# Down weights read two rows to a partition, quarter columns for a lightest expert of up to 32 tokens, and a gather and a code block moved

## The chip, the cores and the metric

One core of a Trainium2 chip runs the whole program. The metric is device time in microseconds (us) of one execution, taken as the median of several. A core has a matrix engine (TensorE, PE in the profile; its weight loads are PEld), a vector engine (DVE), a scalar engine (ACT), GpSimd (POOL) and SyncE (SP), which here issues the weight loads as DMAs. Each engine works through its own list of instructions in order and waits for the others by semaphores.

## The reference, cut to what matters

Two layers act on 256 latent and 256 context tokens of width 1024. The part that the change touches is the channel mixer of the second layer, a SwiGLU with 8 experts of which each of the 256 latent tokens takes two:

```
logits = h @ w_router                       # h: 256 x 1024
top_v, top_i = lax.top_k(logits, 2)
gates = softmax(top_v) spread over the 8 experts, 0 elsewhere
for e in range(8):
    g, u = split(h @ w_gu[e])               # w_gu[e]: 1024 x 7168
    y += gates[:, e:e+1] * ((silu(g) * u) @ w_down[e])   # w_down[e]: 3584 x 1024
```

All is in 32-bit floats. The weights of the 8 experts are 352 MB and are read once.

## The kernel before

The first layer and the attention of the second come first; then the router's logits are made, the experts are sorted by their number of tokens (`sort_experts`; expert 0 is always put first), and `posms` and `gates` hold places and gates by rank. The code then branches. If any expert has more tokens than its rank allows (`odd > 0`), a general path runs (`any_experts`); otherwise `run_pairs` runs. In it the four ranks 0, 2, 3, 1 are "heavy" (up to 128 tokens, `HS`) and ranks 4, 5, 6, 7 are "light" (up to 64 tokens, `LS`), and `schedule` interleaves a heavy and a light one, chunk by chunk: the hidden width 3584 is cut into three chunks of 1024 and one of 512 (`CHUNKS`), and the light one runs one chunk behind. For a chunk there are gate and up products (`Hg`, `Hu`, `Lg`, `Lu`), a transposition of the activations (`Ht`, `Lt`), and in the next slot the down product (`Hd`, `Ld`). The list is cut where rank 1 begins: plan 0 is ranks 0, 2, 3 with 4, 5 and most of 6, plan 1 is rank 1 with the end of 6 and with 7. Between the plans is a second branch: with `k1` over 128 tokens in rank 1, plan 1 runs in its "few" form, in which tokens 129 to 160 of rank 1 are a third group (`few_tokens` gathers them, L1711 and L1781 are its products, 32 columns wide).

Weights come in tiles of 1 MB through a ring of 8 buffers (`raw`), by SP in one queue, in the order of use; SP issues a load when the buffer that it takes is free (L80). A heavy tile is split into a high and a low part by ACT (`whi`, L99) and DVE (`wlo`, L100), three split tiles at most, and takes three products per piece (L537 to L539). A light tile goes into PE unsplit (L1735 gate and up, L1801 down). There two instructions of 64 tokens work side by side on two halves of a chunk's columns. In plan 1 a heavy buffer comes free only after the few product has read it, since `Wb.keep` holds it.

A down tile is 256 rows of 1024 floats, put as rows p and 128+p into partition p. `heavy_turn` and `light_turn` transpose blocks of 128 neighbouring columns of the activations, which are the weights of the down products.

Gathers and the adding of finished experts into `y` (`combine`, L1363) are generators in `bg`, of which a step is run after most operations. The order on PE, DVE and ACT is that of the code in `run_pairs`.

Of the kernel before, what the change touches and what calls it, by code (L numbers as in the profile page):

```python
# [8 lines left out]
F32 = mybir.dt.float32  # L9
# [158 lines left out]
def kernel(ctx: ExitStack, tc: tile.TileContext, x, c, cx, c_ctx, w_ada, b_ada, norm_g,  # L168
# [890 lines left out]
    def pair_items(plan):  # L1059
        r = []  # L1060
        for op, p, c, i in plan:
            l = "l" if op[0] == "L" else "m"
            f0, n = CHUNKS[c]
            for t in range(2 * i, 2 * i + 2):
                if op[1] == "d":
                    f = f0 + 256 * t
                    r.append((tile_of(p, slice(f, f + 256), slice(0, D), w_dn_m, "o (f p) n -> p (o f) n"), l + "d", 2))
                elif op[1] in "gu":
                    q, k = f0 + (FF if op[1] == "u" else 0), 2048 // n
                    r.append((tile_of(p, slice(128 * k * t, 128 * k * t + 128 * k), slice(q, q + n), w_gu_m,  # L1070
                                      "o (k p) n -> p (o k) n"), l + "g", k))
        return r
# [545 lines left out]

    def light_gather(p):
# [29 lines left out]
    def run_pairs(plan, few, todo):  # L1649
# [14 lines left out]
        def few_tokens(p):  # L1664
            sl2 = x2r[:, 0:256].rearrange("p (t n) -> p t n", t=2)
            for t in range(2):
                p2 = tiny([128, 1], "p2")
                V.tensor_scalar(p2, posms[:, t, p:p + 1], -128.0, None, op0=OP.add)
                V.tensor_scalar(sl2[:, t, :].rearrange("p (g n) -> p g n", g=4),
                                iota[:, 0:32].unsqueeze(1).to_broadcast([128, 4, 32]), p2, None, op0=OP.is_equal)  # L1670
            for h in range(2):
                pb, q = hb[h], slice(32 * h, 32 * h + 32)
                for i, (t, src) in enumerate(((0, hth), (0, htl), (1, hth), (1, htl))):
                    PE.matmul(pb, sl2[:, t, :], src[:, t, hsl(h)], start=i == 0, stop=i == 3)
                A.copy(fact[q, :], pb[q, :])
            yield
            pb = tr0[:, 0:256]
            for c in range(4):
                PE.transpose(pb[:, 64 * c:64 * c + 64], fact[0:64, 128 * c:128 * c + 128], ident[0:64, 0:64])
            A.copy(x2.rearrange("p (h c) n -> p c h n", h=2), pb.rearrange("p (c h n) -> p c h n", c=4, h=2))  # L1680
            for t in range(2):
                PE.transpose(facc[:, 128 * t:128 * t + 128], sl2[:, t, :].bitcast(F32), ident)
            A.copy(st2, facc[:, :256])
            yield

        def heavy_gu(p, c, i, up):
            x1, n = XG[p], CHUNKS[c][1]
            nb, w4, per = n // 512, n // 4, 2048 // n
            tokens = few_tokens(p) if few and c == i == 0 and not up else None
            if tokens:  # L1690
                next(tokens)
# [10 lines left out]
            if tokens:  # L1702
                next(tokens)
# [21 lines left out]

        def light_gu(p, c, i, up):
            n = CHUNKS[c][1]
            w2, per = n // 2, 2048 // n
            o = lb[:, 0:w2]
            for t in range(2 * i, 2 * i + 2):  # L1730
                raw = Wb.get("lg")
                for k in range(per):
                    kk = per * t + k
                    for g_ in range(2):
                        PE.matmul(o[64 * g_:64 * g_ + 64, :], X32[p][:, kk, :], raw[:, k, w2 * g_:w2 * g_ + w2],  # L1735
                                  start=kk == 0, stop=kk == KD - 1)
            if i == n // 512 - 1:
                evac(1, [lact[:, 0:w2]], [o], up)

        def heavy_turn(p, c, i):  # L1740
            n = CHUNKS[c][1]
            for b in range(n // 512):
                for k in range(4):
                    q = slice(128 * k, 128 * k + 128)
                    PE.transpose(hb[b][:, q], hact[b][:, q], ident)
                A.copy(th[b], hb[b])
                V.tensor_tensor(tl[b], hb[b], th[b].bitcast(F32), op=OP.subtract)
            if few and p == 1:
                for j in range(n // 512):
                    PE.transpose(tr0[:, 128 * j:128 * j + 128], fact[:, 128 * j:128 * j + 128], ident)  # L1750
                A.copy(t2[:, 0:n // 4], tr0[:, 0:n // 4])

        def light_turn(p, c, i):
            w2 = CHUNKS[c][1] // 2
            for j in range(w2 // 128):
                PE.transpose(lb[:, 128 * j:128 * j + 128], lact[:, 128 * j:128 * j + 128], ident)
            A.copy(lt[:, 0:w2], lb[:, 0:w2])  # L1757
# [35 lines left out]
        def light_down(p, c, i):  # L1793
            nj = CHUNKS[c][1] // 256
            final = c == len(CHUNKS) - 1
            for t in range(2):
                raw = Wb.get("ld")
                for f in range(2):
                    g_, j = divmod(4 * i + 2 * t + f, nj)
                    for h in range(2):  # L1800
                        PE.matmul(lacc[64 * h:64 * h + 64, :], lt[:, 128 * j + 64 * g_:128 * j + 64 * g_ + 64],  # L1801
                                  raw[:, f, hsl(h)], start=c == 0 and i == t == f == 0, stop=final and t == 1 and f == 1)
            if final:
                o = [ring.tile([128, 512], F32R, "x2", i) for i in range(2)]
                split_hl(*o, lacc)
                S_["parts"] = [(SL32[p], in_halves(o))]
# [81 lines left out]
    with odd_arm.Else():  # L1888
# [58 lines left out]
```

## Time and profile before

| | us |
|---|---|
| median of 3 runs (1916.24 to 1918.6) | 1918.11 |
| the profiled execution | 1916.19 |
| its span in the trace | 1914.4 |
| PE busy | 1818.3 (95%) |
| DVE busy | 948.4 (50%) |
| ACT busy | 812.2 (42%) |

Engines overlap, so busy times don't add up to the span. A view of windows gives for each stretch its length, then the busy time and count of instructions of PE, PEld, DVE, ACT and POOL, the granted clock of PE (1.00 is the full 2.4 GHz, 0.5 is 1.2 GHz), the busy share of the 16 DMA engines and the GB/s moved. A share over 1 comes from packets that overlap on an engine. A timeline row is start, duration, engine, line, operation, output and inputs, shapes, count of merged instructions, and in brackets the idle time ahead and what ended it. A wait row is who waited for whom, the total, the times and the longest. A row for one line of the code gives least, median and greatest duration in ns. A q behind an engine means its sequencer.

### The profile page before, as it was taken

The numbers are of one execution on the slowest core, as the hardware profiler recorded it, in microseconds if no ns is written. First come the engines' busy times: TensorE is split into PE (matmuls) and PEld (weight loads), VectorE is DVE, ScalarE is ACT, GpSimd is POOL, SyncE is SP. The second block draws the span as 40 slices with busy tenths as digits, with TensorE's granted clock in tenths as the row PEclk, the third lists the DMA queues.
The fourth block names the chain that finished last, engine by engine and source line by source line (L and its number), as shares of the span: only waits on it lengthen the run. The fifth ranks groups of instructions, "written<-read, shape, count | busy, mean of one in ns | idle before, by whom it ended". The sixth has DMA issues, their size and how long they took to land. (4 is left out here: it accounts for less than half of the span.)

```text
span 1914.4 us, 23955 instructions
## 1 busy us (share of the span) xinstructions
PE 1818.3 (95%) x9321; PEld 1273.7 (67%) x9321; DVE 948.4 (50%) x1310; ACT 812.2 (42%) x1194; POOL 79.0 (4%) x139
## 2 busy tenths in 40 slices
PE   6999999999999999999779999999999996999997
PEld 3866679877777888877666656566565653655553
DVE  3344578322232748536556545665455543545433
ACT  3354457221212547438445535454354443434322
POOL 2200110000000000200200000000000000000001
PEclk9999999999999999999969999999999998999999
DMA  9956286645552656733438999999999998898994
GB/s 337 200 174 203 105 287 209 208 154 176 172 179 89 220 180 235 174 104 111 176 107 339 368 404 404 409 409 406 406 404 409 410 404 349 323 375 334 373 376 187
DMA packets 223760, 521.12 MB, mean 272 GB/s; under 512 B 30040, under 2 KB 83856, under 8 KB 223632
## 3 DMA queue, kind: packets, MB, share of 16 engines
q1 hardware_dynamic: 223152, 519.27, 74.3%
q8 instruction: 77, 1.26, 0.3%
q14 instruction: 51, 0.42, 0.1%
q10 hardware_dynamic: 480, 0.18, 0.0%
HBM read 518.31 MB, written 3.13 MB: 272 GB/s over the span
## 5 line engine op out<-in xcount | busy, mean ns | idle before, releaser
L100 DVE TENSOR_TENSOR wlor<-rawr,whir 128x1024 fp32r<-128x1024 f32 x336 | 395.7, 1221 | 386.3 <-ACT whir L99 375.0
L99 ACT CAST whir<-rawr 128x1024 fp32r<-128x1024 f32 x336 | 335.4, 1049 | 340.9 <-DMA rawr<-in_w_gu_moe_dram 163.1
L100 DVE TENSOR_TENSOR wlo<-raw,whi 128x1024 fp32r<-128x1024 f32 x188 | 224.6, 1222 | 113.6 <-ACT whi L99 74.5
L99 ACT CAST whi<-raw 128x1024 fp32r<-128x1024 f32 x192 | 193.0, 1049 | 143.8 <-PE pg L538 40.3
L1735 PE MATMUL gur<-rawr,x32r 128*64 128x512 f32 (+1 forms) x1024 | 205.1, 547 | 6.5 <-ACT lar L1757 5.3
L537 PE MATMUL gur<-whir,xgr 128*128 128x512 f32 x448 | 181.0, 404 | 11.8 <-issue 6.7
L538 PE MATMUL gur<-wlor,xgr 128*128 128x512 f32 x448 | 176.0, 393 | 0.0
L539 PE MATMUL gur<-whir,xgr 128*128 128x512 f32 x448 | 175.6, 392 | 0.0
L1735 PEld LDWEIGHTS gur<-rawr,x32r 128*64 128x64 f32 x1024 | 69.5, 137 | 118.2 <-issue 100.0
L537 PEld LDWEIGHTS gur<-whir,xgr 128*128 128x128 f32 x448 | 84.9, 190 | 51.1 <-issue 22.0
L1801 PE MATMUL pd<-rawr,lar 128*64 128x512 f32 x448 | 101.7, 598 | 0.5 <-ACT lar L1757 0.5
L539 PEld LDWEIGHTS gur<-whir,xgr 128*128 128x128 f32 x448 | 84.8, 189 | 18.4
L538 PEld LDWEIGHTS gur<-wlor,xgr 128*128 128x128 f32 x448 | 84.9, 189 | 16.0
L537 PE MATMUL pg<-hh,whi 128*128 128x512 f32 (+1 forms) x256 | 95.0, 372 | 0.0
L539 PE MATMUL pu<-hh,wlo 128*128 128x512 f32 (+1 forms) x256 | 93.0, 363 | 0.4 <-DVE wlo L100 0.4
L539 PE MATMUL pg<-hh,wlo 128*128 128x512 f32 (+1 forms) x256 | 93.1, 364 | 0.0
L537 PE MATMUL pu<-hh,whi 128*128 128x512 f32 (+1 forms) x256 | 92.9, 363 | 0.0
L538 PE MATMUL pg<-hl,whi 128*128 128x512 f32 (+1 forms) x256 | 92.9, 363 | 0.0
L538 PE MATMUL pu<-hl,whi 128*128 128x512 f32 (+1 forms) x256 | 92.8, 362 | 0.0
L945 DVE TENSOR_TENSOR act<-sg,pu 128x512 f32<-128x512 f32 (+1 forms) x32 | 19.8, 620 | 147.1 <-PE pu L539 128.7
L537 PE MATMUL py<-whi,ah 128*128 128x512 f32 x224 | 87.4, 390 | 0.0
L539 PE MATMUL py<-whi,al 128*128 128x512 f32 x224 | 86.8, 390 | 0.6 <-DVE al L550 0.6
(391 smaller groups left out, 2972.5 us busy)
## 6 DMA issues: line engine op xcount, KB each, us to landing
rawr<-in_w_gu_moe_dram SPq DMA_DIRECT2D x224, 1024.0 KB
rawr<-in_w_down_moe_dram SPq DMA_DIRECT2D x112, 1024.0 KB
raw<-in_w_ada_dram SPq DMA_DIRECT2D x48, 1024.0 KB
raw<-in_w_gu_dense_dram SPq DMA_DIRECT2D x32, 1024.0 KB
raw<-in_w_down_dense_dram SPq DMA_DIRECT2D x28, 1024.0 KB
raw<-in_w_in_dram SPq DMA_DIRECT2D x24, 1024.0 KB
raw<-in_w_out_dram SPq DMA_DIRECT2D x12, 1024.0 KB
BM<-rep SPq DMA_DIRECT2D x8, 512.0 KB
```

The source lines that it names most:

```text
L99: nc.scalar.copy(hi[:, q], flat[:, q])
L100: (nc.gpsimd if g == "G" else nc.vector).tensor_tensor(lo[:, q], flat[:, q], hi[:, q].bitcast(F32), op=OP.subtract)
L537: PE.matmul(o, wh, mh, start=first, stop=False, skip_group_check=shared)
L538: PE.matmul(o, wh, ml, start=False, stop=False, skip_group_check=shared)
L539: PE.matmul(o, wl, mh, start=False, stop=last, skip_group_check=shared)
L945: V.tensor_tensor(act[f // 4][:, f % 4, s0:s0 + n], sg, pu, op=OP.mult)
L1735: PE.matmul(o[64 * g_:64 * g_ + 64, :], X32[p][:, kk, :], raw[:, k, w2 * g_:w2 * g_ + w2], start=kk == 0, stop=kk == KD - 1)
L1801: PE.matmul(lacc[64 * h:64 * h + 64, :], lt[:, 128 * j + 64 * g_:128 * j + 64 * g_ + 64], raw[:, f, hsl(h)], start=c == 0 and i == t == f ...
```

## The change

1. Down tiles of the chunks of 1024 are read with rows 2p and 2p+1 in partition p, so that a partition's 8 KB is one stretch of memory. To match, the transpositions of those chunks take every second column of a 256-wide block (`block`), not 128 neighbouring ones.
2. If the lightest expert (rank 7) has at most 32 tokens (`k7`), plan 1 is run in a form in which its products use four groups of 32 instead of two of 64 (`groups`, `quarters`). Its gather of tokens is the same (`light_gather`); `quarter_slots` makes the scattering matrix for this form.
3. The gather of the few tokens (`few_tokens`, now `few_gather`) moves from inside the first heavy product of plan 1 to the background of plan 0, behind the gather of rank 7.
4. The branch on `odd` is laid out so that the general path is not the code that follows it.

```diff
-                    r.append((tile_of(p, slice(f, f + 256), slice(0, D), w_dn_m, "o (f p) n -> p (o f) n"), l + "d", 2))
+                    rows_ = "o (p f) n -> p (o f) n" if n == 1024 else "o (f p) n -> p (o f) n"
+                    r.append((tile_of(p, slice(f, f + 256), slice(0, D), w_dn_m, rows_), l + "d", 2))
...
+    LQ = ring.tile([128, 512], F32R, "x2", 3)[:, 0:256]
+
+    def quarter_slots(p):
+
+        sl = LQ.rearrange("p (t n) -> p t n", t=2)
+        for t in range(2):
+            V.tensor_scalar(sl[:, t, :].rearrange("p (g n) -> p g n", g=4),
+                            iota[:, 0:32].unsqueeze(1).to_broadcast([128, 4, 32]), posms[:, t, p:p + 1], None,
+                            op0=OP.is_equal)
+        yield from pause(2)
+        pb = tbank()
+        for t in range(2):
+            PE.transpose(pb[:, 128 * t:128 * t + 128], sl[:, t, :].bitcast(F32), ident)
+        A.copy(LQ, pb[:, :256])
+        yield
...
+    def few_gather(p):
+
+        sl2 = x2r[:, 0:256].rearrange("p (t n) -> p t n", t=2)
+        fact = ring.tile([128, 512], F32, "sg", 1)
+        for t in range(2):
+            p2 = tiny([128, 1], "p2")
+            V.tensor_scalar(p2, posms[:, t, p:p + 1], -128.0, None, op0=OP.add)
...
+        yield from pause(2)
+        for h in range(2):
+            pb, q = tbank(), slice(32 * h, 32 * h + 32)
+            for i, (t, src) in enumerate(((0, hth), (0, htl), (1, hth), (1, htl))):
+                PE.matmul(pb, sl2[:, t, :], src[:, t, hsl(h)], start=i == 0, stop=i == 3)
+            A.copy(fact[q, :], pb[q, :])
+            yield
...
-            tokens = few_tokens(p) if few and c == i == 0 and not up else None
-            if tokens:
-                next(tokens)
...
+        def groups(p):
+
+            return 4 if quarters and p == LS[-1] else 2
+
         def light_gu(p, c, i, up):
-            n = CHUNKS[c][1]
-            w2, per = n // 2, 2048 // n
-            o = lb[:, 0:w2]
+            n, G = CHUNKS[c][1], groups(p)
+            wg, per, m = n // G, 2048 // n, 128 // G
+            o = lb[:, 0:wg]
...
-                    for g_ in range(2):
-                        PE.matmul(o[64 * g_:64 * g_ + 64, :], X32[p][:, kk, :], raw[:, k, w2 * g_:w2 * g_ + w2],
+                    for g_ in range(G):
+                        PE.matmul(o[m * g_:m * g_ + m, :], X32[p][:, kk, 0:m], raw[:, k, wg * g_:wg * g_ + wg],
                                   start=kk == 0, stop=kk == KD - 1)
...
+        def block(a, c, k):
+
+
+            if CHUNKS[c][1] < 1024:
+                return a[:, 128 * k:128 * k + 128]
+            return a[:, 256 * (k // 2):256 * (k // 2) + 256].rearrange("p (n f) -> p f n", f=2)[:, k % 2, :]
...
-                    PE.transpose(hb[b][:, q], hact[b][:, q], ident)
+                    PE.transpose(hb[b][:, q], block(hact[b], c, k), ident)
...
-                        PE.matmul(lacc[64 * h:64 * h + 64, :], lt[:, 128 * j + 64 * g_:128 * j + 64 * g_ + 64],
-                                  raw[:, f, hsl(h)], start=c == 0 and i == t == f == 0, stop=final and t == 1 and f == 1)
+
+                        q = 64 * h + 32 * f if G == 4 else 64 * h
+                        PE.matmul(lacc[q:q + m, :], lt[:, 128 * j + m * g_:128 * j + m * g_ + m], raw[:, f, hsl(h)],
+                                  start=c == 0 and i == t == 0 and (f == 0 or G == 4),
+                                  stop=final and t == 1 and (f == 1 or G == 4))
...
+    k7 = nc.values_load(keyi[0:1, 7:8], min_val=0, max_val=8 * S + 7)
...
-    with tc.If(odd > 0) as odd_arm:
+    with tc.If(odd > 0, preferred_fallthrough_block=False) as odd_arm:
...
-            ("Hg", 2, 3, 0): [lambda: light_gather(6)], ("Hg", 3, 2, 0): [lambda: light_gather(7)]})
+            ("Hg", 2, 3, 0): [lambda: light_gather(6)], ("Hg", 3, 2, 0): [lambda: light_gather(7), lambda: quarter_slots(7), lambda: few_gather(1)]})
...
-            finish(gates[:, :, LS[-1]], run_pairs(plans[1], True, {}))
+            with tc.If(k7 < 8 * 33) as quarter_arm:
+                finish(gates[:, :, LS[-1]], run_pairs(plans[1], True, {}, True))
+            back1()
+            with quarter_arm.Else():
+                finish(gates[:, :, LS[-1]], run_pairs(plans[1], True, {}))
```

How this moves instructions is seen on PE at three places. At the branch on `odd`, PE's list before is this (L1350 is the last transposition of the first gather, L1880 the branch, L1596 the first line of the general path):

```order
L1350 MATMUL pd_7384<-kc,slr_7398 128x128 x2
L1875 TENSOR_LOAD bad
L1876 TENSOR_LOAD keyi
L1880 COMPARE_AND_BRANCH
L1596 TENSOR_LOAD cnt
L1599 COMPARE_AND_BRANCH
```

PE's list at the same branch (now L1913) in the changed kernel; L537 to L539 are the first products of plan 0:

```order
L1351 MATMUL pd_7384<-kc,slr_7398 128x128 x2
L1907 TENSOR_LOAD bad
L1908 TENSOR_LOAD keyi
L1909 TENSOR_LOAD keyi
L1913 COMPARE_AND_BRANCH
L537 MATMUL gur_7409<-whir_7102,xgr_7387 128x512
L538 MATMUL gur_7409<-wlor_7103,xgr_7387 128x512
```

Plan 0 now follows the branch directly, and a third register load, that of `k7`, stands ahead of it. At the branch between the plans PE's list before is this (L1756 is the last transposition of plan 0, L1674 the gather of the few tokens, L537 the first heavy product of rank 1):

```order
L1756 MATMUL gur_7411<-kc,sgr_7401 128x128 x4
L1895 COMPARE_AND_BRANCH
L1674 MATMUL gur_7409<-hth,x2r 128x512
L1674 MATMUL gur_7409<-htl,x2r 128x512
L1674 MATMUL gur_7409<-hth,x2r 128x512
L1674 MATMUL gur_7409<-htl,x2r 128x512
L1674 MATMUL gur_7410<-hth,x2r 128x512
L1674 MATMUL gur_7410<-htl,x2r 128x512
L1674 MATMUL gur_7410<-hth,x2r 128x512
L1674 MATMUL gur_7410<-htl,x2r 128x512
L537 MATMUL gur_7409<-whir_7216,xgr_7387 128x512
```

The same place in PE's list of the changed kernel, where L1784 is that transposition and L1928 and L1929 are the branches on `k1` and `k7`:

```order
L1784 MATMUL gur_7411<-kc,sgr_7401 128x128 x4
L1928 COMPARE_AND_BRANCH
L1929 COMPARE_AND_BRANCH
L537 MATMUL gur_7409<-whir_7216,xgr_7387 128x512
L538 MATMUL gur_7409<-wlor_7217,xgr_7387 128x512
```

The eight gather products are gone from between the branch and the first heavy product. In plan 1, at the first gate product of rank 7, PE's list before is this (L1711 is the few product, L1735 the light one):

```order
L539 MATMUL gur_7410<-whir_7102,xgr_7387 128x512
L1711 MATMUL tr_7382<-rawr_7090,x2f 32x256 x8
L1711 MATMUL tr_7382<-rawr_7092,x2f 32x256 x8
L1735 MATMUL gur_7411<-rawr_7094,x32r_7395 64x512 x4
L1735 MATMUL gur_7411<-rawr_7096,x32r_7395 64x512 x4
L537 MATMUL gur_7409<-whir_7216,xgr_7387 128x512
```

The same place in PE's list of the changed kernel, where L1728 is the few product and L1756 the light one:

```order
L539 MATMUL gur_7410<-whir_7102,xgr_7387 128x512
L1728 MATMUL tr_7382<-rawr_7090,x2f 32x256 x8
L1728 MATMUL tr_7382<-rawr_7092,x2f 32x256 x8
L1756 MATMUL gur_7411<-rawr_7094,x32r_7395 32x256 x8
L1756 MATMUL gur_7411<-rawr_7096,x32r_7395 32x256 x8
L537 MATMUL gur_7409<-whir_7216,xgr_7387 128x512
```

The light product has taken on the shape and count of the few product.

## Rows read from the trace of the kernel before

**Rows 1.** Windows: most of plan 0, two stretches of plan 1, plan 1 whole.

```profile
1100.00:1607.00 507.00, 491.29 (x2247) 301.23 (x2245) 265.65 (x265) 226.35 (x268) 0.00 (x0) 0.99 1.03 406
1620.00:1650.00 30.00, 29.82 (x202) 21.15 (x206) 10.16 (x12) 13.65 (x19) 0.00 (x0) 0.94 0.59 224
1800.00:1870.00 70.00, 69.32 (x456) 38.67 (x456) 25.85 (x27) 22.23 (x28) 0.00 (x0) 1.00 0.98 379
1607.00:1884.00 277.00, 262.15 (x1669) 155.53 (x1667) 126.46 (x129) 105.44 (x129) 0.00 (x0) 0.98 0.92 353
```

**Rows 2.** Waits of all engines in 1100 to 1607 us: ACT for weights.

```profile
ACT whir L99 <- DMA rawr<-in_w_gu_moe_dram: 126.8, 42, 10.0
ACT whir L99 <- DMA rawr<-in_w_down_moe_dram: 100.7, 28, 10.5
```

**Rows 3.** Timeline: the last down product of rank 7.

```profile
1894.90 3.65 PE L1801 MATMUL pd<-rawr,lar 128*64 128x512 f32 x16 [0.46 <-ACT lar L1757]
```

**Rows 4.** Timeline: PE's first product of plan 0.

```profile
982.42 0.79 PE L537 MATMUL gur<-whir,xgr 128*128 128x512 f32 x1 [6.71 <-issue]
```

**Rows 5.** Lines L1880, L1895, L1876: branches and a register load on PE.

```profile
L1880 PEldq COMPARE_BRANCH  x1: 6329/6329/6329, 976.0 to 976.0; - x1
L1895 PEldq COMPARE_BRANCH  x2: 82/1880/3678, 1603.6 to 1901.6; - x2
L1876 PEldq TENSOR_LOAD <-keyi x1: 312/312/312, 975.6 to 975.6; - x1
```

**Rows 6.** DMA queues in 280-300, 1420-1540, 1719.5-1721.5 and 1711-1714 us: packets, MB, share.

```profile
q1 hardware_dynamic: 6100, 6.16, 96.7%
...
DMA packets 12710, 49.08 MB, mean 409 GB/s; under 512 B 747, under 2 KB 747, under 8 KB 12701
q1 hardware_dynamic: 12701, 48.97, 102.5%
...
q14 instruction: 1, 0.01, 1.0%
...
q8 instruction: 1, 0.02, 2.1%
```

**Rows 7.** Timelines of DVE, ACT and PE at the branch between the plans.

```profile
1609.05 0.68 DVE L1747 TENSOR_TENSOR tlr<-gur,thr 128x512 fp32r<-128x512 f32 x1
1609.65 2.35 DVE L100 TENSOR_TENSOR wlor<-rawr,whir 128x1024 fp32r<-128x1024 f32 x2
1617.29 2.36 DVE L100 TENSOR_TENSOR wlor<-rawr,whir 128x1024 fp32r<-128x1024 f32 x2 [5.29 <-ACT whir L99]
1619.57 0.15 DVE L1668 TENSOR_SCALAR p<-posms 128x1 f32<-128x1 f32 x1
...
1616.21 1.99 ACT L99 CAST whir<-rawr 128x1024 fp32r<-128x1024 f32 x2 [5.51 <-DMA rawr<-in_w_gu_moe_dram]
...
1620.09 0.80 PE L1674 MATMUL gur<-hth,x2r 128*128 128x512 f32 x1 [12.24 <-DVE p L1668]
...
1623.60 0.40 PE L537 MATMUL gur<-whir,xgr 128*128 128x512 f32 x1
```

**Rows 8.** Timeline of PE in plan 1: one call each of light and few products.

```profile
1682.15 1.93 PE L1711 MATMUL tr<-rawr,x2f 128*32 128x256 f32 x32
1684.02 3.65 PE L1735 MATMUL gur<-rawr,x32r 128*64 128x512 f32 x16
...
1726.61 1.92 PE L1781 MATMUL pd<-rawr,x2f 128*32 128x512 f32 x16
...
1729.12 3.65 PE L1801 MATMUL pd<-rawr,lar 128*64 128x512 f32 x16
...
1819.06 1.96 PE L1711 MATMUL tr<-rawr,x2f 128*32 128x128 f32 x64
...
1868.08 3.67 PE L1735 MATMUL gur<-rawr,x32r 128*64 128x256 f32 x32 [0.68 <-ACT lar L1757]
```

**Rows 9.** Groups of 1607 to 1900 us by form: weight loads of the heavy transpositions.

```profile
L1745 PEld LDWEIGHTS gur<-kc,actr 128*128 128x128 f32 x28 | 3.1, 140 | 1.5 <-issue 1.2
```

More of the change, by code (lines that the diff above doesn't have):

```diff
@@ L1647, in light_gather, with run_pairs @@
         yield
-    def run_pairs(plan, few, todo):
+    def few_gather(p):
[4 more added lines that the diff above has]
+            V.tensor_scalar(p2, posms[:, t, p:p + 1], -128.0, None, op0=OP.add)
+            V.tensor_scalar(sl2[:, t, :].rearrange("p (g n) -> p g n", g=4),
+                            iota[:, 0:32].unsqueeze(1).to_broadcast([128, 4, 32]), p2, None, op0=OP.is_equal)
+        yield from pause(2)
[5 more added lines that the diff above has]
+            yield
+        pb = tbank()
+        for t in range(2):
+            PE.transpose(pb[:, 128 * t:128 * t + 128], sl2[:, t, :].bitcast(F32), ident)
+        A.copy(x2r[:, 256:512], pb[:, :256])
+        yield
+        pb = tbank()[:, 0:256]
+        for c in range(4):
+            PE.transpose(pb[:, 64 * c:64 * c + 64], fact[0:64, 128 * c:128 * c + 128], ident[0:64, 0:64])
+        A.copy(x2f[:, 0:256].rearrange("p (h c n) -> p c h n", h=2, c=4), pb.rearrange("p (c h n) -> p c h n", c=4, h=2))
+        yield
+    def run_pairs(plan, few, todo, quarters=False):
         arm[0] = "few pair" if few else "pair"
@@ L1662, in run_pairs @@
         st2 = x2r[:, 256:512]
[L1664 to L1684, printed above, removed]
         def heavy_gu(p, c, i, up):
@@ L1701, in heavy_gu @@
                         mm3(hb[b], x1[:, 0, kk, :], x1[:, 1, kk, :], wh[:, k, q], wl[:, k, q], kk == 0, kk == KD - 1)
-            if tokens:
-                next(tokens)
             o2 = tr0[:, 256 * up:256 * up + w4]
@@ L1733, in light_gu @@
                     kk = per * t + k
-                    for g_ in range(2):
-                        PE.matmul(o[64 * g_:64 * g_ + 64, :], X32[p][:, kk, :], raw[:, k, w2 * g_:w2 * g_ + w2],
+                    for g_ in range(G):
+                        PE.matmul(o[m * g_:m * g_ + m, :], X32[p][:, kk, 0:m], raw[:, k, wg * g_:wg * g_ + wg],
                                   start=kk == 0, stop=kk == KD - 1)
             if i == n // 512 - 1:
-                evac(1, [lact[:, 0:w2]], [o], up)
+                evac(1, [lact[:, 0:wg]], [o], up)
+        def block(a, c, k):
+            if CHUNKS[c][1] < 1024:
+                return a[:, 128 * k:128 * k + 128]
+            return a[:, 256 * (k // 2):256 * (k // 2) + 256].rearrange("p (n f) -> p f n", f=2)[:, k % 2, :]
         def heavy_turn(p, c, i):
@@ L1749, in heavy_turn @@
                 for j in range(n // 512):
-                    PE.transpose(tr0[:, 128 * j:128 * j + 128], fact[:, 128 * j:128 * j + 128], ident)
+                    PE.transpose(tr0[:, 128 * j:128 * j + 128], block(fact, c, j), ident)
                 A.copy(t2[:, 0:n // 4], tr0[:, 0:n // 4])
         def light_turn(p, c, i):
[L1754 to L1757, printed above, removed]
+            wg = CHUNKS[c][1] // groups(p)
+            for j in range(wg // 128):
+                PE.transpose(lb[:, 128 * j:128 * j + 128], block(lact, c, j), ident)
+            A.copy(lt[:, 0:wg], lb[:, 0:wg])
         def heavy_down(p, c, i):
@@ L1793, in light_down @@
         def light_down(p, c, i):
-            nj = CHUNKS[c][1] // 256
+            G = groups(p)
+            nj, m = CHUNKS[c][1] // 128 // G, 128 // G
             final = c == len(CHUNKS) - 1
@@ L1805, in light_down @@
                 split_hl(*o, lacc)
-                S_["parts"] = [(SL32[p], in_halves(o))]
+                S_["parts"] = [(LQ if G == 4 else SL32[p], in_halves(o))]
                 if p != LS[-1]:
```

## The prediction

> **What bounds the kernel now.** I first read the windows, to see by stage whether PE or the weight stream sets the pace. From 1100 to 1607 us, most of plan 0, the DMA engines are full (share 1.03, 406 GB/s) and PE is busy for 491.3 of 507 us [rows 1]. That looks like a tie, so I asked for the waits: ACT stood 126.8 + 100.7 us there waiting for weights to land before it could split them [rows 2], so tiles are used as they land, and PE's 15.7 us of idle are what is left of that lateness. Plan 0 goes at the pace of the DMA, with some 3% of PE to spare. In plan 1 it is the other way round: in 1800 to 1870 us PE is busy for 69.3 of 70 us at 379 GB/s, and over the whole of it only 353 GB/s are moved [rows 1], because the few product (L1711, L1781) adds to PE's work for each tile. The last product that needs weights ends at 1894.90 + 3.65 = 1898.5 us [rows 3], and what follows (the rest of the adding, the norm, the store) is not changed. So the question is by how much that moment moves.
>
> Times here are of the profiled execution, 1916.2 us, of which 1914.4 are the span; it is 0.1% under the median of the runs, 1918.1. Runs of this kernel lie within about 0.1%, so I take 0.2% (some 4 us) as what can be told from no change.
>
> **The branch on `odd`.** PE waits 6.71 us ahead of its first product of plan 0, for nothing but its own issue, and the reason is one row: its compare-and-branch took 6.329 us, where the branch between the plans, whose wanted code stands right behind it, took 0.082 [rows 4, 5]. In the new order plan 0 stands behind the branch. This takes off 6.33 - 0.08, and the register load for `k7` puts back 0.31 [rows 5]: **-5.9 us**. The wait was for issue alone, so the operands were there and nothing else takes its place. SP loads when PE frees a buffer, so the whole of plan 0 moves with it. Bounds: 0, if something unseen holds PE, to -6.3.
>
> **The down rows.** There are 96 tiles affected (8 experts x 3 chunks x 4), 68 in plan 0, 28 in plan 1. Their packets, pieces that a DMA engine moves in one go, become 8 KB instead of 4 KB. The trace has no row for such a load, so I price packets by size. 6100 packets of about 1 KB took 96.7% of 20 us on 16 engines, 50.7 ns each; in a stretch of 4 KB packets 12701 - 747 took 102.5% of 120 us on 16 engines, less 747 tiny ones of some 10 ns, 164 ns each [rows 6]. That makes 37.8 ns for a KB and 13 ns for a packet. A tile is 16 packets of 4 KB on each engine, then 8 of 8 KB: 8 x 13 = 0.10 us less of 2.57 (1.05 MB at 409 GB/s). An 8 KB packet should then take 315 ns; the one that I can see, which fetched instructions, took 1.0% of 2 us on 16 engines, 320 ns [rows 6]. For 64 tiles of plan 0 (four come before the DMA is full) this gives -6.7, in plan 1 -2.9. Bounds for plan 0: 0, if the packets stay at 4 KB, to -6.7. I take **-4**, because PE has only those 15.7 us to spare there and gets more to do, next.
>
> The Trainium skill, in "DMA: Bandwidth & Descriptors", section "Why small descriptors are slow (HBM only)", gives a packet a fixed cost of about 3 bus cycles of 32 bytes each. By it 8 KB would be 259 cycles against 262, 1.1% less, an estimate, and all 96 tiles would save 2.9 us instead of 9.6. The slope in the rows is over three times that, and the rows decide.
>
> **The strided blocks.** 144 transpositions (96 heavy, 42 light, 6 few) now load weights for PE with every second float. No row shows such a load; the nearest takes 140 ns [rows 9]. Bounds: 0, to twice as long, 144 x 0.14 = 20 us of which those of plan 0 (two thirds) would mostly lie in PE's spare time, so +7 at the end. I take 0, since weight loads run beside products and PEld is busy for only 155.5 of the 277 us of plan 1 [rows 1].
>
> The Trainium skill, in "SBUF — State Buffer", section "Door 1: The DMA port swizzle", says that SBUF is read in lines of 16 bytes and that up to four 32-bit floats may be stepped over for free. By it the term is 0; no run here shows it yet.
>
> **The gather moved into plan 0.** It brings eight products, two pairs of transpositions and some ACT copies, and `quarter_slots` a pair more: some 3 us of PE at full clock. Cover is PE's 15.7 us of idle [rows 1]; without it the price is those 3 plus a wait or two for ACT's copies, +5. I take **+1**. It issues no DMA.
>
> **The start of plan 1.** PE idles 12.24 us before the gather. It waits for DVE's L1668, which stands in DVE's list behind the split (L100) of a tile that had only just landed, at 1616.2 [rows 7]. That tile is the third of rank 1; the first product doesn't need it. Without the gather PE can start when its bank is free, at 1609.05 + 0.68 = 1609.7 (the first tile's split had then ended, the second's ends at 1612.0). Before, it started at 1623.60 [rows 7]: 13.8 us, and the gather's transpositions later in that product take another 0.9. But the DMA ran on during the wait and then stood with full buffers (224 GB/s in 1620 to 1650 [rows 1]), so PE loses the lead that it had been given.
>
> **The quarters.** Whether the form runs depends on the inputs: the reference's router on them gives 138 tokens to rank 1 and 96, 71, 45, 43, 28 and 26 to the ranks behind, so the 26 of rank 7 fit. The shape of its new products is that of the few product, which has rows: a gate or up call of 16 instructions takes 3.65 us now, one of 32 quarters 1.93; the small chunk 3.67 against 1.96; a down call 3.65 against 1.92 [rows 8]. Rank 7 has 12 + 2 + 7 = 21 calls, so 21 x 1.72 = 36.1 us of PE less. (Seven transpositions fewer are under a microsecond more, left out.)
>
> **The sum for plan 1.** PE alone: 13.8 + 0.9 + 36.1 = 50.8, so its end moves from 1898.5 to 1847.7. The DMA alone: 353 GB/s over 277 us is 97.8 MB [rows 1]; at plan 0's 406 GB/s they take 240.9 us, ending at 1847.9, less 2.9 for the longer rows, and about 2 from the last landing to the last product: 1847. Two limits at the same place with eight buffers between them cost something: fed like this in plan 0, PE idled 3.1%, which is 7.5 us of 240. PE's end is then 1855, without it 1848; I take 1853, nearer to the dearer one, because the buffers are held longer here than in plan 0: **-45.5**.
>
> Sum: 1916.2 - 5.9 - 4 + 1 - 45.5 = 1861.8, so **1862 us**, 2.9% under the run it is made from.
>
> **The rivals.**
> *The buffers keep the DMA from filling.* In plan 1 a heavy buffer is held until the few product has read it, and even its best long stretch moved 379 GB/s [rows 1]. At that rate 97.8 MB end at 1865, or 1864 with the last product and the longer rows, so -34.5 instead of -45.5: 1873. For it: SP's loads would still hang on L1711. Against it: 379 was set by PE being full, not by the DMA.
> *The longer rows give nothing.* 4 in plan 0 and 2 to 3 in plan 1 come back: 1868. By the skill's price above it would be about 1866.
> *The strided loads cost double.* +7: 1869.
> *Slower: longer packets run worse.* A 16 KB packet, also of instructions, took 2.1% of 3 us on 16 engines, 1.0 us [rows 6], 61 ns for a KB instead of 40. If rows of 8 KB ran like that, each tile would take 64 KB x 21 ns = 1.3 us more on each engine; all of it lies in stretches where the DMA is full, 96 x 1.3 = 129 us: 1991. It decides from 0.57 us a tile on, an 8 KB packet of about 390 ns; the one in the rows had 320, which speaks against it.
> *The quarters don't run.* Then PE jumps far once more (+6.3) and only the start of plan 1 is won: 1916.2 - 5.9 - 4 + 1 - 14.7 + 6.3 = 1899. Only another count of tokens would do this.
>
> **How the numbers follow.** Forecast (1850 to 1868): 0.58. Buffers: 0.18. Rows give nothing: 0.10. Strided loads: 0.04. Longer packets worse: 0.04. No quarters: 0.01. The remaining 0.05 is for an end before 1850, where the lost 7.5 us don't appear and the longer rows count in full. The range 1848 to 1882 leaves out the slow packets, the missing quarters, some of the early ends and the worst of the buffers, together under 2 in 10. All cases but the slow packets are faster by over 0.2%: faster 0.95, the same 0.01, slower 0.04.
>
> **What would show it.** PE's branch on `odd` under 0.2 us. In plan 0, packets of down tiles near 315 ns and a higher rate than 406 GB/s, with plan 0 ending some 9 us earlier. PE's first product of rank 1 within 3 us of the last transposition of plan 0. L1756 calls of rank 7 of 1.9 us. Plan 1 with a DMA share near 1 and PE idle for a few per cent. The forecast is wrong if PE stays full in plan 1 (then a call costs more than its rows), if the DMA share there stays at 0.95 while PE idles (the buffers), or if packets of 8 KB take over 330 ns.

## The result and the profile after

The changed kernel took **1883.55 us** (median of 4 runs, 1882.4 to 1885.01) against 1918.36 of the kernel before on the same chip: ratio 0.9821, 95% interval 0.9804 to 0.9838. It is faster by 34.8 us, where 54 were forecast; 1883.55 lies just above the range. The profiled execution took 1884.5 us, its span 1882.7.

First the windows of the changed kernel: plan 0 where the DMA is full, five stretches of plan 1 from heavy transposition to heavy transposition (the last one to the last down product), and plan 1 up to 1850.

```profile
core 0: us, PE busy (x) PEld busy (x) DVE busy (x) ACT busy (x) POOL busy (x), PEclk, DMA share, GB/s
1100.00:1590.00 490.00, 472.23 (x2165) 292.76 (x2164) 259.62 (x264) 223.42 (x266) 0.00 (x0) 0.99 1.02 409
1606.70:1659.00 52.30, 52.30 (x363) 34.82 (x362) 28.39 (x29) 24.20 (x30) 0.00 (x0) 1.00 0.94 360
1659.00:1718.40 59.40, 57.78 (x459) 37.84 (x458) 30.32 (x30) 24.61 (x29) 0.00 (x0) 1.00 1.01 400
1718.40:1775.60 57.20, 56.31 (x461) 37.28 (x460) 29.61 (x29) 25.20 (x30) 0.00 (x0) 1.00 0.95 374
1775.60:1837.90 62.30, 53.59 (x436) 33.83 (x435) 23.86 (x25) 18.16 (x23) 0.00 (x0) 0.84 0.94 370
1837.90:1866.70 28.80, 24.41 (x253) 13.51 (x250) 9.27 (x11) 7.31 (x12) 0.00 (x0) 0.94 0.80 311
1606.70:1850.00 243.30, 228.10 (x1861) 149.60 (x1863) 117.59 (x118) 97.45 (x119) 0.00 (x0) 0.95 0.96 377
```

Beside [rows 1]: plan 0 is as full as before, at 409 instead of 406 GB/s. In plan 1 PE is nearly full for three stretches; in the fourth and fifth it is idle for 8.7 and 4.4 us and its granted clock falls to 0.84 and 0.94, while the DMA moves less than in plan 0.

PE's branch on `odd` and the branches between the plans (L1929's second execution is on the way out), then PE's first product of plan 0, in the changed kernel:

```profile
L1913 PEldq COMPARE_BRANCH  x1: 98/98/98, 977.7 to 977.7; - x1
L1928 PEldq COMPARE_BRANCH  x1: 68/68/68, 1603.1 to 1603.1; - x1
L1929 PEldq COMPARE_BRANCH  x2: 67/1864/3662, 1603.3 to 1869.7; - x2
```

```profile
977.88 0.78 PE L537 MATMUL gur<-whir,xgr 128*128 128x512 f32 x1 [0.96 <-issue]
```

The 6329 ns of [rows 5] are 98, and the idle of 6.71 us in [rows 4] is 0.96. The start of plan 0 moved by 4.5 us, not 5.8, since the work ahead of the branch ended 1.2 us later in this execution.

The gather in its new place, by the timelines of ACT, DVE and PE in the changed kernel, with the transpositions ahead of it and at the end of plan 0:

```profile
1575.65 1.99 ACT L99 CAST whir<-rawr 128x1024 fp32r<-128x1024 f32 x2 [9.92 <-DMA rawr<-in_w_down_moe_dram]
...
1576.72 2.36 DVE L100 TENSOR_TENSOR wlor<-rawr,whir 128x1024 fp32r<-128x1024 f32 x2 [10.32 <-ACT whir L99]
1579.00 0.15 DVE L1672 TENSOR_SCALAR p<-posms 128x1 f32<-128x1 f32 x1
...
1545.35 1.12 PE L1773 MATMUL gur<-kc,actr 128*128 128x128 f32 x8
1579.53 0.80 PE L1679 MATMUL pd<-hth,x2r 128*128 128x512 f32 x1 [6.52 <-DVE p L1672]
1606.70 0.75 PE L1784 MATMUL gur<-kc,sgr 128*128 128x128 f32 x4
1607.20 0.47 PE L537 MATMUL gur<-whir,xgr 128*128 128x512 f32 x1
```

This is the stall of [rows 7] over again: DVE's four mask instructions stand behind the split of a tile that has only just landed, and PE's gather behind DVE. From that heavy transposition to the last one of plan 0 PE took 61.35 us, where it had taken 53.56 (1553.64 to 1607.20 in the trace before). The start of the stretch is 8.3 us earlier, its end 0.5. Rank 1 then begins 0.5 us behind that last transposition, where it had begun 16.4 behind it (1607.20 to the 1623.60 of [rows 7]).

The last down product, the wait for weights in the fourth stretch (ACT's and PE's timelines), and plan 1's calls for rank 7, in the changed kernel:

```profile
1864.73 1.92 PE L1832 MATMUL pd<-rawr,lar 128*32 128x512 f32 x16 [0.41 <-ACT lar L1785]
...
1810.24 1.99 ACT L99 CAST whir<-rawr 128x1024 fp32r<-128x1024 f32 x2 [12.02 <-DMA rawr<-in_w_down_moe_dram]
...
1805.09 3.70 PE L1756 MATMUL gur<-rawr,x32r 128*32 128x256 f32 x64
1811.34 0.50 PE L537 MATMUL pdn0r<-whir,thr 128*128 128x512 f32 x1 [2.55 <-ACT whir L99]
1812.60 0.79 PE L538 MATMUL pdn0r<-wlor,thr 128*128 128x512 f32 x1 [0.76 <-DVE wlor L100]
1813.19 0.63 PE L539 MATMUL pdn0r<-whir,tlr 128*128 128x512 f32 x1
```

A call of quarters takes 1.85 to 1.92 us (3.70 for two), half of [rows 8]. Work that needs weights ends at 1866.65 instead of 1898.55. The products at 1813 take 0.63 us, where others take 0.39. The window of these products shows why:

```profile
1812.60:1815.20 2.60, 2.60 (x6) 2.11 (x7) 2.60 (x4) 2.00 (x2) 0.00 (x0) 0.50 1.01 419
```

The granted clock is 0.50, the lower of PE's two levels (1.2 GHz), after the waits of 2.55 and 0.76 us. In 1803 to 1808 us, ahead of them, it was 1.00. So a wait for weights costs PE more than its own length.

Weight loads of the transpositions of 1607 to 1900 us, and the DMA packets of 1420 to 1540 us, in the changed kernel:

```profile
L1773 PEld LDWEIGHTS gur<-kc,actr 128*128 128x128 f32 x28 | 3.7, 197 | 1.4 <-issue 1.2
```

```profile
DMA packets 11315, 49.41 MB, mean 412 GB/s; under 512 B 753, under 2 KB 753, under 8 KB 9697
## 3 DMA queue, kind: packets, MB, share of 16 engines
q1 hardware_dynamic: 11309, 49.33, 102.1%
```

A load with every second float takes 197 ns, the plain one of [rows 9] 140. With 164 ns for each of the 9697 - 753 packets of 4 KB, as in [rows 6], some 302 ns are left for each of 1612 packets of 8 KB (315 were reckoned).

### The profile page after: what moved, and what is told of

Same layout as the page of the kernel before. It is cut to its first block, busy times and chain, and to the rows that moved or that the text cites. A ratio compares the mean times of both kernels' runs of the same rounds, so it can differ in the third digit from the quotient of the medians.

```text
span 1882.7 us, 24473 instructions
## 1 busy us (share of the span) xinstructions
PE 1790.2 (95%) x9572; PEld 1275.9 (68%) x9572; DVE 948.3 (50%) x1312; ACT 810.4 (43%) x1195; POOL 78.7 (4%) x139
## 5 line engine op out<-in xcount | busy, mean ns | idle before, releaser
L1756 PE MATMUL gur<-rawr,x32r 128*64 128x512 f32 (+3 forms) x1280 | 182.2, 476 | 7.7 <-ACT lar L1785 4.2
L537 PE MATMUL gur<-whir,xgr 128*128 128x512 f32 x448 | 181.5, 405 | 5.2 <-DVE tlr L1775 4.2
L539 PE MATMUL gur<-whir,xgr 128*128 128x512 f32 x448 | 176.0, 393 | 0.0
L1756 PEld LDWEIGHTS gur<-rawr,x32r 128*64 128x64 f32 (+1 forms) x1280 | 68.8, 129 | 99.4 <-issue 73.6
L537 PEld LDWEIGHTS gur<-whir,xgr 128*128 128x128 f32 x448 | 85.2, 190 | 41.1 <-issue 11.8
L539 PEld LDWEIGHTS gur<-whir,xgr 128*128 128x128 f32 x448 | 85.1, 190 | 18.5
L537 PE MATMUL pg<-hh,whi 128*128 128x512 f32 (+1 forms) x256 | 95.0, 372 | 0.0
L539 PE MATMUL pu<-hh,wlo 128*128 128x512 f32 (+1 forms) x256 | 93.0, 363 | 0.4 <-DVE wlo L100 0.4
L539 PE MATMUL pg<-hh,wlo 128*128 128x512 f32 (+1 forms) x256 | 93.1, 364 | 0.0
L537 PE MATMUL pu<-hh,whi 128*128 128x512 f32 (+1 forms) x256 | 92.9, 363 | 0.0
L1832 PE MATMUL pd<-rawr,lar 128*64 128x512 f32 (+1 forms) x448 | 91.2, 614 | 0.4 <-ACT lar L1785 0.4
L537 PE MATMUL py<-whi,ah 128*128 128x512 f32 x224 | 87.4, 390 | 0.0
L539 PE MATMUL py<-whi,al 128*128 128x512 f32 x224 | 86.8, 390 | 0.6 <-DVE al L550 0.6
```

What stands on the lines that cost most here:

```text
L537: PE.matmul(o, wh, mh, start=first, stop=False, skip_group_check=shared)
L539: PE.matmul(o, wl, mh, start=False, stop=last, skip_group_check=shared)
L1756: PE.matmul(o[m * g_:m * g_ + m, :], X32[p][:, kk, 0:m], raw[:, k, wg * g_:wg * g_ + wg], start=kk == 0, stop=kk == KD - 1)
L1832: PE.matmul(lacc[q:q + m, :], lt[:, 128 * j + m * g_:128 * j + m * g_ + m], raw[:, f, hsl(h)], start=c == 0 and i == t == 0 and (f == 0 or ...
```

## The experiments

Beside the medians, one length is read from each trace: from the start of plan 0's last transposition to the end of the last down product of rank 7. It is 259.95 us in the changed kernel (1606.70 to 1866.65), 291.35 before; the forecast had 245.8. Theory A: PE's work and the weight stream limit plan 1 one after the other, PE first, and the weights that did not come in the meantime are waited for in the fourth and fifth stretch. Two executions of the same code differ by 3.6 us in this length (kernel 8 below), so smaller differences in it tell little. The rivals stand in the expectations: what is short lies elsewhere, in PE's own work, in the buffers or in another term of the sum.

**1. Half of each late load.** The last 32 tiles are loaded by half; the rest of each buffer holds old data, so the output lacks these halves.

```diff
-            self.nc.sync.dma_start(t, ap)
+            if isinstance(self, Mixed) and self.ri >= 304:
+                self.nc.sync.dma_start(t[:, 0:a // 2], ap[:, 0:a // 2])
+            else:
+                self.nc.sync.dma_start(t, ap)
```

> Of the last 32 weight tiles (those of the last two slots of plan 1) only half of each is loaded, so part of the products use old data; every instruction of PE, ACT and DVE stays. Theory A (the weight stream runs out of lead: in the first three slots of plan 1 it stands with full buffers because PE is full, and in the last two PE starves): the slot that took 62.3 us falls to 45 to 50, the last one from 28.7 to about 24, and the time falls by 14 to 20 us, to 1864 to 1870. Theory B (PE itself is dearer in those slots: its granted clock fell to 0.84 and the quarter calls cost more there): the slot stays at 57 or more and the time at 1878 or more.

Measured: 1866.97 us, ratio 0.9742 (0.9725 to 0.9758). Windows of this kernel, the fourth stretch and plan 1:

```profile
1775.10:1820.90 45.80, 44.65 (x435) 29.30 (x434) 23.06 (x25) 16.84 (x22) 0.00 (x0) 1.00 0.65 230
1606.70:1850.00 243.30, 236.37 (x1965) 152.91 (x1964) 121.72 (x125) 100.00 (x124) 0.00 (x0) 0.99 0.85 324
```

The fourth stretch falls from 62.3 to 45.8 us and the clock stays at 1.00; the last, expected at 24, still takes 27.4 (28.8 before the halving). The length is 242.5 us (1605.77 to 1848.31), and of the 6.9 us that PE idles in it only 0.7 wait for a split. That is PE alone, 240.5 in the forecast. So PE's work was sized rightly, and weights are what is waited for.

**2 to 4. One suspected cost each.** In 2 the four mask instructions on DVE are made one call earlier, at the gather of rank 6; in 3 each few product stands directly behind its heavy tile, which frees the buffer of the first of two sooner; in 4 rank 7 keeps its two halves.

```diff
-("Hg", 2, 3, 0): [lambda: light_gather(6)], 
+("Hg", 2, 3, 0): [lambda: light_gather(6), lambda: few_masks(1)], 
```

```diff
             for t in range(2 * i, 2 * i + 2):
                 wh, wl = Wb.get("mg")
...
+                if few:
+                    for k in range(per):
...
-            if few:
-                for t in range(2 * i, 2 * i + 2):
-                    for k in range(per):
```

```diff
-                finish(gates[:, :, LS[-1]], run_pairs(plans[1], True, {}, True))
+                finish(gates[:, :, LS[-1]], run_pairs(plans[1], True, {}, False))
```

> Only the four DVE instructions that make the masks of the few tokens move, to a place some 250 us earlier; the gather's products stay where they are. Theory A (the wait of 6.5 us for DVE in the gather, and the half clock behind it, moved the start of plan 1 back by some 8 us): the wait is gone, plan 1 starts 5 to 9 us earlier and the time falls by 4 to 8 us, to 1876 to 1880. Rival (the weight stream is the limit anyway, so what PE wins there it loses later): the start moves, the time stays within 2 us of 1883.5.

> In plan 1 the few product of a heavy tile follows right behind that tile's heavy product instead of behind both tiles' products, so one buffer of two comes free some 4 us earlier. Theory A (held buffers keep the weight stream from running ahead in the first three slots): the stream gains one tile of lead, 2 to 3 us, and moves more than 378 GB/s over plan 1; the time falls by 1 to 4 us, to 1880 to 1882. Rival (holding has no part in it, PE's pace alone frees buffers): no change within 1 us, or 1 to 2 us slower by the twice as many changes between 128 and 32 columns on PE.

> The changed kernel with the light products of rank 7 in two groups of 64 again; all else as changed. Theory A (36 us of PE's work were taken out, but some 20 of them turned into waiting for weights): the time rises by only 14 to 20 us, to 1898 to 1904, with PE full all through plan 1 and the clock at 1.00. Theory B (the quarters cost PE more than their rows): it rises by less than 12 us. If the quarters had been worth their full 36 us, it would rise to 1919.

Measured: 2: 1879.3 us, 0.9802 (0.9783 to 0.9821). 3: 1880.66, 0.9807 (0.979 to 0.9823). 4: 1900.88, 0.9912 (0.9896 to 0.9929). PE's timeline in 2, the gather and the last transposition of plan 0, then the window of plan 1 in 4:

```profile
1575.96 0.50 PE L1684 MATMUL pd<-hth,x2r 128*128 128x512 f32 x1
...
1603.20 0.75 PE L1789 MATMUL gur<-kc,sgr 128*128 128x128 f32 x4
```

```profile
1606.70:1850.00 243.30, 242.78 (x1549) 143.76 (x1547) 116.23 (x115) 95.09 (x114) 0.00 (x0) 1.00 0.94 363
```

The gather no longer waits, and plan 0 ends 3.5 us sooner (5 to 9 were expected), which reaches the end. Of the 7.8 us that the stretch with the gather grew by, about half is thus that wait. Kernel 3's gain of 2.9 lies at the edge of what can be told; its length is 259.4, hardly less. With two halves (4) PE is full again and the time 17.3 us longer: the quarters give half of the 36.1 us that they take from PE.

**5 to 7. One part of the change undone.** In 5 the down rows stand as before and the blocks are unstrided, in 6 plan 0 is again the far side of the branch, in 7 the gather is back at the start of plan 1.

```diff
-rows_ = "o (p f) n -> p (o f) n" if n == 1024 else "o (f p) n -> p (o f) n"
+rows_ = "o (f p) n -> p (o f) n"
...
```

```diff
-    with tc.If(odd > 0, preferred_fallthrough_block=False) as odd_arm:
+    with tc.If(odd > 0) as odd_arm:
```

```diff
-lambda: quarter_slots(7), lambda: few_gather(1)]})
+lambda: quarter_slots(7)]})
...
+            tokens = few_tokens(p) if few and c == i == 0 and not up else None
+            if tokens:
+                next(tokens)
```

> The changed kernel with the down tiles in 4 KB rows again (and blocks of neighbouring columns to match); all else as changed. Theory A (longer packets save 0.1 us a tile wherever the stream sets the pace, that is in plan 0 and again in the last two slots): the time rises by 5 to 8 us, to 1888 to 1892, with packets of 164 ns and 406 GB/s in plan 0. Rival (PE's own lack of spare time takes the gain, or the dearer strided weight loads of 195 against 140 ns eat it): within 2 us of 1883.5.

> The changed kernel with the general path behind the branch on odd again, so that PE jumps. Theory A (PE sets the pace at the start of plan 0 and everything behind moves with it): the branch takes some 6.3 us again and the time rises by 5 to 6 us, to 1888 to 1890. Rival (the stream that is full later takes the loss up): a rise of less than 2 us.

> The changed kernel with the few tokens' gather between the branch and the first heavy product of rank 1 again. Theory A (a wait of PE ahead of plan 1 costs its length until the stream is the limit, and the move only won the difference between the wait there and the one that it brought to plan 0): plan 0 ends some 6 to 8 us earlier, PE then waits 12 us and makes the gather, and the time rises by 3 to 8 us, to 1887 to 1891. Rival (the stream runs on through the wait and all of it is regained in the last slots): within 2 us of 1883.5.

Measured: 5: 1888.06 us, 0.986 (0.983 to 0.9891). 6: 1891.4, 0.9867 (0.9837 to 0.9897). 7: 1888.31, 0.9853 (0.9825 to 0.9882). Undoing them costs 4.5, 7.9 and 4.8 us; kernel 6 is 1.4 us over what was expected. With the 17.3 of kernel 4 that is 34.5 of the 34.8 us won. PE's timelines, the first product of plan 0 in 6 and the gather in 7:

```profile
984.02 0.79 PE L537 MATMUL gur<-whir,xgr 128*128 128x512 f32 x1 [6.97 <-issue]
```

```profile
1612.40 0.79 PE L1718 MATMUL gur<-hth,x2r 128*128 128x512 f32 x1 [11.74 <-DVE p L1712]
```

The branch is worth its whole price. For the other two, plan 0 is measured from its first product to its last transposition: 624.8 us before, 628.8 in the changed kernel (628.4 to 629.6 in 1, 3, 4, 6, 8, 9 and 10, which have the same plan 0), 634.65 in 5 (974.35 to 1609.00), 620.25 in 7 (979.66 to 1599.91), 624.2 in 2 (978.99 to 1603.20). So rows and blocks together win 4.5 us there (7 against the kernel before) to 5.8 (5 against the changed kernel); the gather costs 8.6, and the masks made earlier give 4.6 of it back. The 4.8 us of kernel 7 are therefore a difference: in its old place the gather spares plan 0 its 8.6 us, but PE waits 11.74 us for DVE, and the length is 275.1 us (1599.91 to 1875.04), 15.2 more than in the changed kernel. The DMA goes on during that wait, but nothing of it is seen to come back.

**8 and 9. A buffer less.** Kernel 8 asks for loads seven tiles ahead instead of eight. Kernel 9 loads only seven of the eight buffers in the quarter form.

```diff
+                Wb.ahead = RAW_N - 1
```

```diff
+                Wb.pool = deque([ring.tiles["raw", (at + j) % RAW_N] for j in range(RAW_N - 1)])
...
+            if self.pool:
+                t = self.pool.popleft()
+                self.pool.append(t)
```

> The changed kernel with one buffer less in use by the weight stream in plan 1 (7 of 8). Theory A (the lead that the stream can build up while PE is full is the number of buffers, and what it lacks it pays for in the last two slots): one tile less of lead, 2.6 us, so the time rises by 2 to 5 us, to 1886 to 1888, and the share of the DMA in the first three slots falls. Rival (the lead is never used up; the last slots are long for another reason): within 1 us.

> In the quarter form of plan 1 only seven of the eight buffers are loaded, so SP really stands for a buffer one tile (2.6 us) sooner. Theory A (in the first three slots PE sets the pace and the DMA stands with full buffers; the weights that are then missing are waited for in slots 4 and 5): a lead of one tile less is lost once where PE begins to wait, so 2 to 5 us over the changed kernel's 1883.6, 1885 to 1889, and slot 4 is the longer by it. Rival B (buffers don't matter, since the DMA's own rate in plan 1 is what is short): within 1 us of 1883.6.

Measured: 8: 1883.68 us, 0.9835 (0.9805 to 0.9864), no change. The edit did not do what it was meant to: SP's loads keep their order and their buffers, and SP waits for the buffer, not for the place in the code. It tells nothing of the buffers, but it is the changed kernel measured a second time: its length is 256.3 us (1608.10 to 1864.42). 9: 1890.71, 0.9858 (0.9843 to 0.9873), 7.2 us slower, more than theory A's 2 to 5; its length is 267.6 (1605.68 to 1873.26). Windows of 9, the last of them plan 1 to 1850, then the same short stretches of the changed kernel:

```profile
1640.00:1645.00 5.00, 5.00 (x47) 3.27 (x46) 2.71 (x4) 0.07 (x1) 0.00 (x0) 1.00 0.46 152
...
1725.00:1730.00 5.00, 5.00 (x56) 3.33 (x58) 4.77 (x5) 2.58 (x3) 0.00 (x0) 1.00 0.19 44
...
1790.00:1795.00 5.00, 5.00 (x98) 3.95 (x100) 0.00 (x0) 1.40 (x3) 0.00 (x0) 1.00 0.68 209
...
1606.70:1850.00 243.30, 222.35 (x1794) 144.18 (x1792) 114.13 (x115) 95.00 (x116) 0.00 (x0) 0.98 0.94 366
```

```profile
1640.00:1645.00 5.00, 5.00 (x47) 3.29 (x46) 1.69 (x3) 1.05 (x1) 0.00 (x0) 1.00 0.90 357
...
1725.00:1730.00 5.00, 5.00 (x71) 2.92 (x70) 3.34 (x3) 1.13 (x2) 0.00 (x0) 1.00 0.31 76
...
1790.00:1795.00 5.00, 5.00 (x95) 3.99 (x97) 2.36 (x2) 3.10 (x5) 0.00 (x0) 1.00 0.37 105
```

In the first two of these places the DMA stands longer with a buffer less, in the third less long, with PE full each time; over plan 1 to 1850 it moves 366 GB/s instead of 377, while PE is idle for 21 us instead of 15.2. So the two limits alternate within plan 1, and a tile of lead is lost more than once. The expectation's rival, that buffers don't matter, falls; so does theory A's "once". The prediction's own rival on the buffers gains by it.

**10. The stream with less for PE to do.** The few product keeps the first piece of each tile in gate and up, and 64 of 512 columns in down; its part of the output is left out.

```diff
-                    for k in range(per):
-                        kk = per * t + k
                         for g_ in range(4):
...
+                            m = 512 if first or last else 64
+                            PE.matmul(facc[q2:q2 + 32, 0:m], t2[:, 128 * j + 32 * g_:128 * j + 32 * g_ + 32],
```

> The few product keeps only the first piece of each tile in gate and up and 64 of 512 columns in down (its part of the output is not computed), so PE has some 26 us less to do in plan 1, while every load, and the order in which the buffers are read, stay. Theory A (weights limit what is left over from a stretch in which PE set the pace): with PE out of the way the DMA can be full throughout, 95 MB at 405 to 409 GB/s from 1606 us, so the last product ends at 1845 to 1850 instead of 1866.6, and the time is 1862 to 1868. Rival B (the held buffers keep plan 1's stream at 378 GB/s whatever PE does): the time stays within 5 us of the changed kernel's 1883.6.

Measured: 1876.94 us, 0.9786 (0.9771 to 0.9801): 6.6 under the changed kernel, between the two expectations. Windows of 10, plan 1 to 1850 and from there to the end of the last product, and its last product:

```profile
1606.70:1850.00 243.30, 216.43 (x1628) 144.18 (x1626) 119.49 (x121) 98.75 (x122) 0.00 (x0) 0.95 1.00 392
...
1850.00:1857.20 7.20, 6.79 (x46) 2.27 (x43) 1.50 (x2) 0.27 (x1) 0.00 (x0) 1.00 0.10 27
```

```profile
1855.23 1.92 PE L1832 MATMUL pd<-rawr,lar 128*32 128x512 f32 x16 [0.41 <-ACT lar L1783]
```

The DMA is nearly full here (1.00 against 0.96), so the held buffers don't fix its rate at 378; but theory A's 405 to 409 is not reached either. From the last weights (near 1851) to the last product it takes some 6 us, not 2. The length is 251.3 us (1605.84 to 1857.15), 8.6 under the changed kernel's. What keeps it from 409 GB/s is seen in two shorter windows of 10, and in what SP waited for most in 1600 to 1860 us (L1726 is the few product of 10):

```profile
1720.00:1725.00 5.00, 5.00 (x59) 3.10 (x58) 4.15 (x4) 1.95 (x3) 0.00 (x0) 1.00 0.41 110
...
1740.00:1760.00 20.00, 17.87 (x160) 11.61 (x152) 10.64 (x12) 6.84 (x8) 0.00 (x0) 1.00 1.02 420
```

```profile
SPq L80 <- PE tr L1726: 84.7, 14, 8.1
```

In the first, the DMA stands for buffers while PE is full: SP's longest wait for the few product, 8.1 us, ends there, at 1722.7. In the second it moves 420 GB/s. By windows of 1 us, from the start of the length to 7 us before its end, the DMA's share is under 0.9 in 17 windows of kernel 10, 29 of the changed kernel and 36 of kernel 9; what the share lacks of 1 there adds up to 6.5, 14.5 and 21.5 us, and PE is busy throughout in all of these windows. In the rest the DMA moves 407, 407 and 405 GB/s, as in plan 0 (410). So the stream is not slower in plan 1, it stands: in kernel 10 too, which is therefore not the stream alone. Less what is lacking, the length is 245 to 246 us in all three (and in 8), and up to 251 in the others.

**11 and 12. Both mends; plain blocks.** Kernel 11 is 2 and 3 together. Kernel 12 keeps the 8 KB rows and reads neighbouring columns, which pairs rows of the down product wrongly.

```diff
-            if CHUNKS[c][1] < 1024:
-                return a[:, 128 * k:128 * k + 128]
-            return a[:, 256 * (k // 2):256 * (k // 2) + 256].rearrange("p (n f) -> p f n", f=2)[:, k % 2, :]
+            return a[:, 128 * k:128 * k + 128]
```

> The masks of the gather made earlier and each few product directly behind its tile, both together. Alone they gave 1879.3 and 1880.7 against 1883.6. If they act at different places (the end of plan 0; slot 4) they add up: 1875 to 1878. If both only shorten the same wait for weights in slots 4 and 5: 1879 to 1880.5.

> The rows of 8 KB stay, but the transpositions read 128 neighbouring columns again (so the down products take the wrong rows). If the strided weight loads, 195 ns instead of 140, cost time on the path: 1 to 2 us less than 1883.6. If they are hidden or only filled by waits for weights: within 1 us.

Measured: 11: 1879.45 us, 0.9799 (0.9783 to 0.9816), runs from 1874.5 to 1883.7. 12: 1880.15, 0.98 (0.9784 to 0.9817). Kernel 11 is the best version that computes the whole output, together with 2, from which it can't be told apart: freeing the first of two buffers sooner added nothing that can be told. Both beat the kernel before clearly, and the changed one by some 4 us, at the edge of what can be told (the runs of 11 overlap with its runs). Kernel 12's gain of 3.4 us is within what can't be told. By PE's groups from 978 us on, its transpositions, changed kernel first, then 12:

```profile
L1773 PE MATMUL gur<-kc,actr 128*128 128x128 f32 x112 | 16.1, 284 | 1.1 <-DVE actr L1739 1.1
L1784 PE MATMUL gur<-kc,sgr 128*128 128x128 f32 x49 | 9.6, 306 | 0.0
```

```profile
L1771 PE MATMUL gur<-kc,actr 128*128 128x128 f32 x112 | 15.2, 274 | 1.1 <-DVE actr L1739 1.1
L1782 PE MATMUL gur<-kc,sgr 128*128 128x128 f32 x49 | 8.5, 284 | 0.0
```

The strides cost PE 0.9 + 1.1 = 2.0 us of its time at most.

## Why the prediction was off, step by step

The direction, the parts and PE's durations were right; the sum was 22.5 us too low: by it the last down product ends at 1898.5 - 5.9 - 4 + 1 - 45.5 = 1844.1, and it ended at 1866.65. The miss is in two places, 8.4 us ahead of plan 1 (1598.3 forecast, 1606.7 measured) and 14.1 in it (245.8 against 259.95).

- **The branch on `odd`, -5.9:** right; the idle fell by 5.75, and undoing it cost 7.9. In the profiled execution plan 0 began only 4.5 us earlier, 1.4 of the 8.4; among the kernels with this order its start lies anywhere from 974.0 to 979.7.
- **The down rows, -4:** right; 4.5 to 5.8 in plan 0, and undoing them cost 4.5. The Trainium skill, "DMA: Bandwidth & Descriptors", section "Why small descriptors are slow (HBM only)", gives about 2.8 us for all 96 tiles by an estimate (the prediction's 2.9, worked out again); what plan 0 alone won is over that, and the slope of the rows was the better price.
- **The strided blocks, 0:** wrong in kind, small in size. The loads take 197 instead of 140 ns, and the transpositions 2.0 us of PE. By the Trainium skill, "SBUF — State Buffer", section "Door 1: The DMA port swizzle", such a step would be free; the trace of these loads does not agree.
- **The gather moved into plan 0, +1:** the first failed step. It was costed as PE's work under PE's idle time. What stands on DVE was left out of the count: the masks came behind a split that waited for weights, 6.52 us for PE, and the first products of the gather at 0.63 us. It measured +8.6 (kernel 7), and the masks made earlier give back 4.6; the 7.6 over the forecast are nearly all of the miss ahead of plan 1. What makes up the other 4.0 us was not taken apart.
- **The start of plan 1, -13.8 and -0.9:** right; with the gather back (kernel 7) the length grows by 15.2.
- **The quarters, -36.1:** right as PE's time, and the shape was priced right. 17.3 reached the end.
- **The sum for plan 1:** the main failed step, in the price of the two limits meeting. PE alone: 240.5 forecast, 242.5 measured (kernel 1). The DMA alone: 239.8 forecast; no kernel shows it, but the 96.0 MB of the five stretches at 407 GB/s and 6 us to the last product make some 242, an estimate. That this comes so near is partly luck: the forecast had 1.8 MB too many and 4 us too few behind the last weights. For the meeting 5.3 us over the larger limit were allowed, taken from plan 0, where PE idles 3.1% and the DMA hardly ever stands (0 of 507 us before, 1.2 of 490 after). In plan 1 the limits alternate: the DMA stands for 14.5 us while PE is full, PE then idles for 15.2 us, and the length is 259.95, 17.4 over the larger limit (13.8 in the execution of kernel 8). The larger limit's 2.0 and the meeting's 17.4 - 5.3 = 12.1 make the 14.1.

The rival "the buffers keep the DMA from filling" came nearest. Its sign in the prediction, a DMA share of 0.95 while PE idles, is what the trace shows: 0.96, with PE idle for 15.2 of 243.3 us. It had 379 GB/s for plan 1, and 377 were measured; with the 8.4 us ahead of plan 1, its 1873 is 1881. Kernel 9 shows that the number of buffers sets the time. But 379 is no rate of the DMA: it is 407 with pauses, and the same buffers, read in the same order, let through 392 where PE has less to do. Whether the few product's hold on two buffers is what counts stays open: kernel 3 frees the first of them sooner, and its length is 259.4.

## What to carry to other kernels

When two limits come out nearly equal in a stage, don't take the price of their meeting from another stage: look in short windows whether each of them stands while the other sets the pace. If they alternate, what each loses adds up; here one buffer of eight was worth 7 us. To see the other limit, thin out one engine's work in that stage before the gain is counted. A step that is moved under another's idle time must be followed on each engine that it touches; here four instructions of 0.15 to 0.29 us on DVE stood behind a wait for weights and took PE with them. Put such small preparations a whole call ahead of their use.

## What was not expected of the hardware

- A weight load for PE that takes every second float: 197 ns instead of 140.
- PE's products behind a wait for weights ran at a granted clock of 0.50; over the fourth stretch, with its 8.7 us of idle, it was 0.84, and 1.00 in the same stretch of kernel 1.
- A taken branch cost PE 6.33 us in [rows 5], the same branch not taken 0.098.
